# An FFN whose half-size weight sums move from VectorE to accumulating transfers of GpSimd

## The chip, the cores and the metric

The kernel runs on one core of one Trainium2 chip. The metric is the device time of one execution in microseconds (us). Before the change, three runs took 1903.16, 1903.44 and 1905.04 us; the median is 1903.44 us.

## The reference, cut to what matters

Two layers, each of which runs a half-step FFN, a set of token mixers and a second half-step FFN on a residual stream `x` of 512 tokens by 1024 features, all in float32. Only the FFN is touched by the change:

```
def swiglu(h, w_in, w_out):
    gate, up = jnp.split(h @ w_in, 2, axis=-1)
    return (jax.nn.silu(gate) * up) @ w_out

x = x + 0.5 * swiglu(rms_norm(x, ffn1_norm[l]), ffn1_w_in[l], ffn1_w_out[l])   # w_in 1024 x 5632, w_out 2816 x 1024
x = x + ...                                                                    # token mixers
x = x + 0.5 * swiglu(rms_norm(x, ffn2_norm[l]), ffn2_w_in[l], ffn2_w_out[l])
```

So there are four FFNs in an execution: first and second FFN of layer 0, first and second FFN of layer 1.

## The kernel before, in words

**Precision.** Every large product is made of three multiplications in a reduced float32 format (fp32r): each operand is split into a rounded part ("hi") and the rest ("lo"), and `mm3` (L208, L212, L213) adds hi·hi, hi·lo and lo·hi. A weight tile is split by `parted`: ScalarE (ACT) casts it to hi (L196), VectorE (DVE) subtracts to get lo (L197). The split tiles `hl` rotate through three buffers, so a split can start when the product three places earlier has ended.

**The FFN's stages.** The 22 blocks of 128 hidden features are taken in chunks of 8, 8 and 6 (`CHUNKS`). For each chunk the kernel computes the hidden activations `hh`, `hl` and then streams `w_out` rows (granules `st`, two buffers) to add the chunk's part of the output into `xT`. In the first chunk of an FFN, `cover` computes 6 blocks (4 in the first FFN of layer 1) with plain products, straight from the unnormalised x; meanwhile `halves_of_x` prepares seven combinations of quarters of the normalised x (tiles `xc`, from `xn` and `T`). From then on `halved` computes the remaining blocks two at a time, as a **pair**, with seven half-size products in the place of eight (the Strassen-Winograd scheme). This makes 12 `halved` stages, of 1 or 2, 4 and 3 pairs: 33 pairs in all. The four stages of an FFN's first chunk are called the **openings** here; they start while `cover`'s last results are still being finished (`finish`: L434 to L440).

**A pair.** A pair needs four quarters of `w_in`, 128 x 1024 floats (512 KB) each, called q0 (gate columns, first half of rows; `a11`), q1 (gate, second half; `a12`), q2 (up, first half; `a21`), q3 (up, second half; `a22`). `load` brings them from HBM with four DMAs on SyncE's queue (SP, L510) into tiles `w`, whose tags `x0`..`x3` and `x4`..`x7` alternate from pair to pair; in an opening the same tags hold the split x that `cover` still multiplies with, so each load starts when `cover` has done with its tag. `combine` makes four sums of quarters on DVE (L529) in tiles `S` (three buffers):

```
1: lambda: (a21, a22, ALU.add),
2: lambda: (s(1), a11, ALU.subtract),
3: lambda: (a11, a21, ALU.subtract),
4: lambda: (a12, s(2), ALU.subtract),
```

The seven products run in the order P1, P2, P6, P5, P7, P3, P4; their weights are q0, q1, sum 2, sum 1, sum 3, sum 4, q3. Each is 24 multiplications of 128 x 128 by 128 x 256. `prepare` splits the weights of a product two products ahead (`LEAD = 2`). Sums 1 and 2 of the next pair are made in the steps P7 and P3, sums 3 and 4 just before their own splits. The results leave PSUM by ACT copies (L583, L589, L592), DVE adds (L585, L594, L596) and `y`, `hh`, `hl` (L602 to L605).

**What sets the order.** The framework's scheduler places instructions on each engine by a simulated time, so the order on a queue need not be that of the source; each engine, and each of the queues SP and GpSimd (POOL), then runs its own list strictly in order. POOL does almost nothing in the kernel before: a few memsets and 16 small DMAs (`og`, `qkg`, `fb`, `cw`, L672 to L678) at the start of the mixers.

Of the kernel before, what the change touches and what calls it, by code (L numbers as in the profile page):

```python
# [8 lines left out]
F32 = mybir.dt.float32  # L9
# [4 lines left out]
AF = mybir.ActivationFunctionType  # L14
ALU = mybir.AluOpType
# [8 lines left out]
P = 128  # L24
# [3 lines left out]
KD = D // P  # L28
FF = 2816
# [15 lines left out]
class Trunk:  # L45
# [268 lines left out]
    def ffn(self, w_in, w_out, next_gain, covered, begin=None, out=None):  # L314
# [5 lines left out]
        with tc.tile_pool(name=self.n("ffn"), bufs=1) as fp:  # L320
# [3 lines left out]
            for f0, nf in CHUNKS:  # L324
# [5 lines left out]
                ]  # L330
                halved = self.halved(fp, w_in, f0 + (covered if f0 == 0 else 0), f0 + nf, f0)
                finish = self.cover(fp, w_in, covered, begin, halved) if f0 == 0 else None
                for n, _ in enumerate(halved):

                    if f0 == 0 and n == 0:
                        finish()
# [105 lines left out]
    def halves_of_x(self, fp):  # L442


        nc = self.nc
        H = T // 2
        xn = []
        for q in range(4):
            xq = fp.tile([P, 2, T], F32, tag=("hh2", "hl2", "hh3", "hl3")[q], name=self.n("xn"))
            for i in range(2):  # L450
                k = 2 * q + i
                nc.vector.scalar_tensor_tensor(  # L452
                    out=xq[:, i, :], in0=self.xT[:, k, :], scalar=self.gain[:, k : k + 1],
                    in1=self.inv, op0=ALU.mult, op1=ALU.mult,
                )
            xn.append(xq)

        quarter = lambda a, b: [xn[2 * a + i][:, :, b * H : (b + 1) * H] for i in range(2)]
        both = lambda t: [t[:, 2 * i : 2 * i + 2, :] for i in range(2)]

        def minus(out, a, b):
            for o, u, v in zip(out, a, b):
                nc.vector.tensor_sub(o, u, v)
            return out

        self.xc = {}

        def part(name, src):
            c = len(self.xc)
            hi, lo = (  # L470
                fp.tile([P, 4, H], F32R, tag=f"x{w}{c}", name=self.n("xc")) for w in "hl"
            )
            for h, l, u in zip(both(hi), both(lo), src):
                nc.scalar.copy(h, u)
                nc.vector.tensor_sub(l, u, h)  # L475
            self.xc[name] = hi, lo

        b11, b12, b21, b22 = (quarter(a, b) for a in range(2) for b in range(2))
        yield part("P1", b11)
        yield part("P2", b21)  # L480
        t1 = both(fp.tile([P, 4, H], F32, tag="S", name=self.n("T"), bufs=3))
        minus(t1, b12, b11)

        t2 = minus(b11, b22, t1)
        yield part("P6", t2)
        yield part("P5", t1)
        yield part("P7", minus(b12, b22, b12))
        yield part("P3", b22)
        yield part("P4", minus(b21, b21, t2))

    def halved(self, fp, w_in, fa, fb, f0):

        nc = self.nc
        H = T // 2
        ORDER = ("P1", "P2", "P6", "P5", "P7", "P3", "P4")  # L500
        steps = [(f, p) for f in range(fa, fb, 2) for p in ORDER]
        raw, sums, parts = {}, {}, {}

        def load(f):
            for q in range(4):
                t = self.res.tile(
                    [P, 4, 2 * P], F32, tag=f"x{4 * ((f - fa) // 2 % 2) + q}", name=self.n("w")
                )
                c = (q // 2) * FF + f * P
                nc.sync.dma_start(  # L510
                    t,
                    w_in[(q % 2) * 512 : (q % 2) * 512 + 512, c : c + 2 * P].rearrange(
                        "(k p) c -> p k c", p=P
                    ),
                )
                raw[f, q] = t

        def combine(f, name):
            a11, a12, a21, a22 = (raw[f, q] for q in range(4))
            s = lambda i: sums[f, i]  # L520

            t = s(2) if name == 4 else fp.tile([P, 4, 2 * P], F32, tag="S", name=self.n("S"), bufs=3)
            a, b, op = {
                1: lambda: (a21, a22, ALU.add),
                2: lambda: (s(1), a11, ALU.subtract),
                3: lambda: (a11, a21, ALU.subtract),
                4: lambda: (a12, s(2), ALU.subtract),
            }[name]()
            nc.vector.tensor_tensor(t, a, b, op=op)  # L529
            sums[f, name] = t  # L530

        def prepare(f, p):
            a11, a12, a21, a22 = (raw[f, q] for q in range(4))
            if p in ("P7", "P3"):
                combine(f, 3 if p == "P7" else 4)
            src = {
                "P1": a11, "P2": a12, "P6": sums.get((f, 2)), "P5": sums.get((f, 1)),
                "P7": sums.get((f, 3)), "P3": sums.get((f, 4)), "P4": a22,
            }[p]
            hi, lo = self.parted(src.rearrange("p k c -> p (k c)"), skew=SKEW_HELD)  # L540
            parts[f, p] = [a.rearrange("p (k c) -> p k c", k=4) for a in (hi, lo)]

        def product(f, p, bank, first, last, parted):
            hi, lo = parts.pop((f, p))
            xh, xl = self.xc[p]
            for i in range(2):
                acc, c = bank[:, i * H : (i + 1) * H], slice(i * P, (i + 1) * P)
                for k in range(4):
                    self.mm3(
                        acc, hi[:, k, c], lo[:, k, c], xh[:, k, :], xl[:, k, :],  # L550
                        first and i == 0 and k == 0, last and i == 1 and k == 3,
                        parted and i == 0 and k == 0,
                    )

        tmp = lambda tag: fp.tile([P, T], F32, tag=tag, name=self.n(tag), bufs=2)
        LEAD = 2
        load(fa)
        for f, p in steps[:LEAD]:
            prepare(f, p)
        yield  # L560
        for n, (f, p) in enumerate(steps):
            if p == "P1" and f == fa:
                combine(f, 1)
                combine(f, 2)
            if n + LEAD < len(steps):
                prepare(*steps[n + LEAD])
            if f + 2 < fb:
                if p == "P1":
                    load(f + 2)
                elif p in ("P7", "P3"):  # L570
                    combine(f + 2, 1 if p == "P7" else 2)
            if p == "P1":
                self.ntog += 1
                a, b, c = (
                    self.bank(t) for t in (("mm", "mm", "mm"), ("sc", "sc", "pt"))[self.ntog % 2]
                )
            product(
                f, p, {"P2": c, "P5": b, "P3": b}.get(p, a), p in ("P1", "P2", "P5"),
                p in ("P2", "P3", "P4"), n == 0,
            )  # L580
            if p == "P1":
                g1 = tmp("g1")
                nc.scalar.copy(g1, a)  # L583
            elif p == "P2":
                nc.vector.tensor_add(g1, g1, c)  # L585
                self.act(g1, g1, AF.Silu)
            elif p == "P6":
                g2 = tmp("g2")
                nc.scalar.copy(g2, a)  # L589
            elif p == "P5":  # L590
                u2 = tmp("u2")
                nc.scalar.copy(u2, b)  # L592
            elif p == "P7":
                nc.vector.tensor_add(u2, u2, a)  # L594
            elif p == "P3":
                nc.vector.tensor_add(g2, g2, b)  # L596
                self.act(g2, g2, AF.Silu)
            else:
                q = (f - f0) // 2
                pair = lambda t: t.rearrange("p (i t) -> p i t", i=2)  # L600
                y = fp.tile([P, 2, T], F32, tag="S", name=self.n("y"), bufs=3)
                nc.vector.tensor_mul(y[:, :, H:], pair(g2), pair(u2))  # L602
                nc.vector.tensor_mul(y[:, :, :H], pair(g1), pair(a))
                nc.scalar.copy(self.hh[q], y)
                nc.vector.tensor_sub(self.hl[q], y, self.hh[q])  # L605
            yield
# [722 lines left out]
```

## Time and profile before

| what | value |
|---|---|
| the profiled execution's own time | 1903.5 us |
| its span (first to last instruction) | 1901.7 us |
| granted TensorE clock | 1.0 |
| PE busy | 1877.0 us (99%) |
| DVE busy | 1390.4 us (73%) |
| ACT busy | 928.7 us (49%) |
| POOL busy | 27.4 us (1%) |
| moved by DMA | 185.63 MB, mean 98 GB/s |

The profiled execution lies 0.06 us from the median of the runs. An engine's busy time is the union of its instructions; for PE the ends of multiplications are modelled, so that its idle gaps are real, but being busy is not being at full speed. "Idle before" in a group of instructions is idle time of that engine just ahead of them, with what ended it.

### The profile page before, as it was taken

How to read it: one execution, taken by the hardware profiler on the slowest of the kernel's cores; microseconds unless marked ns; L12 is line 12 of the kernel's file. 1: busy time of each engine (PE TensorE's matmuls, PEld its weight loads, DVE VectorE, ACT ScalarE, POOL GpSimd, SP SyncE). 2: the span in 40 equal slices, each digit the busy share in tenths (PEclk: the TensorE clock that was granted, in tenths of full speed). 3: DMA queues.
4: the chain of work that ended last, by engine and by line, in shares of the span. 5: the costliest groups of instructions: out<-in, count | busy, mean ns of one | idle time of the engine just before them, and what ended most of it. 6: DMA issues, size and time to landing. Idle time of an engine off the chain costs nothing.

```text
span 1901.7 us, 30176 instructions
## 1 busy us (share of the span) xinstructions
PE 1877.0 (99%) x12240; PEld 1679.9 (88%) x12240; DVE 1390.4 (73%) x2004; ACT 928.7 (49%) x1418; POOL 27.4 (1%) x56
## 2 busy tenths in 40 slices
PE   8999999999999999999999999999999999999999
PEld 6889989899877788989989899998998787899897
DVE  7958757678787884857689486676868878768483
ACT  4525425464666542534555253455546665335252
POOL 0000000100000000000000000001000000000000
PEclk9999999999999999999999999999999999999999
DMA  5442421232323362341244334113323234424302
GB/s 144 145 150 72 145 76 36 73 96 69 77 76 93 99 197 80 100 142 37 73 144 139 100 100 133 45 56 78 91 62 87 78 107 131 159 68 126 106 23 89
DMA packets 176059, 185.63 MB, mean 98 GB/s; under 512 B 17680, under 2 KB 148752, under 8 KB 175920
## 3 DMA queue, kind: packets, MB, share of 16 engines
q1 hardware_dynamic: 175408, 183.69, 32.4%
q8 instruction: 96, 1.57, 0.3%
q14 instruction: 43, 0.35, 0.1%
q0 software_dynamic: 512, 0.02, 0.1%
HBM read 176.27 MB, written 2.10 MB: 94 GB/s over the span
## 4 chain that ended last, share of the span: by engine, by line
PE 84%; DVE 11%; ACT 3%; issue 2%; DMA 0%; SPq 0%; DVEq 0%; ACTq 0%
PE mm L208 13%; PE mm L213 13%; PE mm L212 13%; PE sc L208 8%; PE sc L212 8%; PE sc L213 8%; PE pt L208 4%; PE pt L212 4%; PE pt L213 4%; DVE hl L197 2%; DVE xc L475 2%; PE po L208 1%; PE po L213 1%; PE po L212 1%; DVE xn L452 1%
## 5 line engine op out<-in xcount | busy, mean ns | idle before, releaser
L197 DVE TENSOR_TENSOR hl<-st,hl 128x512 fp32r<-128x512 f32 (+2 forms) x268 | 254.8, 952 | 221.5 <-ACT hl L196 220.5
L196 ACT CAST hl<-st 128x512 fp32r<-128x512 f32 (+2 forms) x268 | 222.4, 832 | 379.0 <-PE pt L213 131.3
L213 PE MATMUL mm<-xc,hl 128*128 128x256 f32 x952 | 263.1, 277 | 2.2 <-DVE hl L197 2.2
L208 PE MATMUL mm<-xc,hl 128*128 128x256 f32 (+1 forms) x958 | 263.5, 276 | 1.7 <-ACT hl L196 1.7
L212 PE MATMUL mm<-xc,hl 128*128 128x256 f32 x952 | 263.1, 276 | 0.0
L208 PE MATMUL sc<-xc,hl 128*128 128x256 f32 (+1 forms) x774 | 212.4, 276 | 0.0
L212 PE MATMUL sc<-xc,hl 128*128 128x256 f32 x768 | 212.3, 276 | 0.0
L213 PE MATMUL sc<-xc,hl 128*128 128x256 f32 x768 | 212.1, 276 | 0.0
L196 ACT CAST hl<-S 128x1024 fp32r<-128x1024 f32 x132 | 138.7, 1051 | 140.1 <-DVE S L529 61.2
L197 DVE TENSOR_TENSOR hl<-w,hl 128x1024 fp32r<-128x1024 f32 x99 | 121.3, 1225 | 110.8 <-ACT hl L196 110.8
L197 DVE TENSOR_TENSOR hl<-S,hl 128x1024 fp32r<-128x1024 f32 x132 | 161.2, 1222 | 29.4 <-ACT hl L196 29.2
L208 PEld LDWEIGHTS mm<-xc,hl 128*128 128x128 f32 x958 | 179.8, 188 | 2.8 <-ACT hl L196 2.3
L213 PEld LDWEIGHTS mm<-xc,hl 128*128 128x128 f32 x952 | 178.6, 188 | 2.9 <-DVE hl L197 2.8
L212 PEld LDWEIGHTS mm<-xc,hl 128*128 128x128 f32 x952 | 178.7, 188 | 0.0
L196 ACT CAST hl<-w 128x1024 fp32r<-128x1024 f32 x99 | 103.9, 1050 | 143.4 <-PE po L213 52.7
L208 PEld LDWEIGHTS sc<-xc,hl 128*128 128x128 f32 x774 | 145.3, 188 | 0.5
L212 PEld LDWEIGHTS sc<-xc,hl 128*128 128x128 f32 x768 | 144.2, 188 | 0.0
L213 PEld LDWEIGHTS sc<-xc,hl 128*128 128x128 f32 x768 | 144.2, 188 | 0.0
L208 PE MATMUL mm<-hl,x 128*128 128x256 f32 (+1 forms) x384 | 112.4, 293 | 0.7 <-DVE qk L1105 0.4
L208 PE MATMUL mm<-x,hl 128*128 128x512 f32 x272 | 109.9, 404 | 0.0
L213 PE MATMUL mm<-hl,x 128*128 128x256 f32 (+1 forms) x384 | 107.5, 280 | 0.0
L212 PE MATMUL mm<-hl,x 128*128 128x256 f32 (+1 forms) x384 | 107.3, 279 | 0.0
(407 smaller groups left out, 4640.5 us busy)
## 6 DMA issues: line engine op xcount, KB each, us to landing
w<-in_ffn_w_in_dram SPq DMA_DIRECT2D x132, 512.0 KB, 3.6
st<-in_ffn_w_out_dram SPq DMA_DIRECT2D x88, 512.0 KB, 3.4
st<-in_ffn_w_in_dram SPq DMA_DIRECT2D x88, 256.0 KB, 3.2
st<-in_w_mix_in_dram SPq DMA_DIRECT2D x88, 256.0 KB, 2.7
st<-in_w_mix_out_dram SPq DMA_DIRECT2D x24, 256.0 KB, 2.8
st<-in_w_mix_in_dram SPq DMA_DIRECT2D x32, 128.0 KB, 2.3
xs<-in_x_dram SPq DMA_DIRECT2D x8, 256.0 KB, 5.5
QB<-QA SPq DMA_DIRECT2D x16, 128.0 KB, 2.3
```

Source lines behind the costliest of these rows:

```text
L196: a = nc.scalar.copy(hi, src[:, c : c + w])
L197: b = nc.vector.tensor_sub(lo, src[:, c : c + w], hi)
L208: nc.tensor.matmul(acc[:, c], ah, bh[:, c], start=first and c.start == 0, stop=False, skip_group_check=True,)
L212: nc.tensor.matmul(acc, ah, bl, start=False, stop=False, skip_group_check=True)
L213: nc.tensor.matmul(acc, al, bh, start=False, stop=last, skip_group_check=True)
L452: nc.vector.scalar_tensor_tensor(out=xq[:, i, :], in0=self.xT[:, k, :], scalar=self.gain[:, k : k + 1], in1=self.inv, op0=ALU.mult, op1=AL ...
L475: nc.vector.tensor_sub(l, u, h)
```

## The change

Three of the four sums of a pair are made by transfers that GpSimd issues with `accum_op=ALU.add`: the transfer reads its source and adds it to what the destination holds. `load` brings the quarters in the order q2, q3, q0, q1 and then has q3 read once more from HBM and added onto the tile of q2 (sum 1: q2 + q3). `second` is the one sum left on DVE (tile `S`): that sum + q0. `third` reads q2 once more from HBM and adds it onto the tile of q0, after q0 has been split for P1 and read by `second`. `fourth` adds the tile `S` onto the tile of q1, after q1 has been split for P2 (from SBUF to SBUF).

As these transfers can only add, signs are moved into x: the first four of the eight blocks of x in `halves_of_x` are multiplied by a negated gain (`ngain`, one small ACT instruction for each FFN), two of its combinations change their form, and three ACT copies out of PSUM get a factor of -1. The products, their order, the DMAs of `load` (but for their order) and everything outside the four FFNs stay as they are. `combine` goes, and with it three of four L529 instructions.

```diff
         xn = []
+        self.ngain = self.const.tile([P, KD], F32, tag="ngain", name=self.n("ngain"))
+        nc.scalar.activation(self.ngain, self.gain, AF.Copy, scale=-1.0)
...
-                    out=xq[:, i, :], in0=self.xT[:, k, :], scalar=self.gain[:, k : k + 1],
+                    out=xq[:, i, :], in0=self.xT[:, k, :],
+                    scalar=(self.ngain if k < 4 else self.gain)[:, k : k + 1],
...
-        t2 = minus(b11, b22, t1)
+        t2 = minus(b11, b22, t1, ALU.add)
...
-        yield part("P7", minus(b12, b22, b12))
+        yield part("P7", neither(b12, b12, b22))
...
         def load(f):
-            for q in range(4):
+            for q in (2, 3, 0, 1):
...
-        def combine(f, name):
...
+            nc.gpsimd.dma_start(raw[f, 2], quarter(f, 3), accum_op=ALU.add)
+
+        def second(f):
+            t = sums[f] = fp.tile([P, 4, 2 * P], F32, tag="S", name=self.n("S"), bufs=3)
+            nc.vector.tensor_add(t, raw[f, 2], raw[f, 0])
+
+        def third(f):
+            nc.gpsimd.dma_start(raw[f, 0], quarter(f, 2), accum_op=ALU.add)
+
+        def fourth(f):
+            nc.gpsimd.dma_start(raw[f, 1], sums[f], accum_op=ALU.add)
+
         def prepare(f, p):
-            if p in ("P7", "P3"):
-                combine(f, 3 if p == "P7" else 4)
             src = {
-                "P1": a11, "P2": a12, "P6": sums.get((f, 2)), "P5": sums.get((f, 1)),
-                "P7": sums.get((f, 3)), "P3": sums.get((f, 4)), "P4": a22,
+                "P1": raw[f, 0], "P2": raw[f, 1], "P6": sums.get(f), "P5": raw[f, 2],
+                "P7": raw[f, 0], "P3": raw[f, 1], "P4": raw[f, 3],
             }[p]
...
             if p == "P1" and f == fa:
-                combine(f, 1)
-                combine(f, 2)
+                second(f)
+            if p == "P1":
+                third(f)
+                fourth(f)
...
-                elif p in ("P7", "P3"):
-                    combine(f + 2, 1 if p == "P7" else 2)
+                elif p == "P7":
+                    second(f + 2)
...
-                nc.scalar.copy(g1, a)
+                nc.scalar.activation(g1, a, AF.Copy, scale=-1.0)
```

The same replacement of a copy by a copy times -1 is made for `g2` and `u2`.

More of the change, by code (lines that the diff above doesn't have):

```diff
@@ L459, in halves_of_x, with minus, neither @@
         both = lambda t: [t[:, 2 * i : 2 * i + 2, :] for i in range(2)]
-        def minus(out, a, b):
+        def minus(out, a, b, op=ALU.subtract):
             for o, u, v in zip(out, a, b):
-                nc.vector.tensor_sub(o, u, v)
+                nc.vector.tensor_tensor(o, u, v, op=op)
+            return out
+        def neither(out, a, b):
+            for o, u, v in zip(out, a, b):
+                nc.vector.scalar_tensor_tensor(
+                    out=o, in0=u, scalar=-1.0, in1=v, op0=ALU.mult, op1=ALU.subtract
+                )
             return out
@@ L502, in halved, with quarter @@
         raw, sums, parts = {}, {}, {}
+        def quarter(f, q):
+            c = (q // 2) * FF + f * P
+            return w_in[(q % 2) * 512 : (q % 2) * 512 + 512, c : c + 2 * P].rearrange(
+                "(k p) c -> p k c", p=P
+            )
         def load(f):
-            for q in range(4):
+            for q in (2, 3, 0, 1):
                 t = self.res.tile(
@@ L508, in load @@
                 )
[L509 to L515, printed above, removed]
-                raw[f, q] = t
-        def combine(f, name):
[L519 to L530, printed above, removed]
+                nc.sync.dma_start(t, quarter(f, q))
+                raw[f, q] = t
+            nc.gpsimd.dma_start(raw[f, 2], quarter(f, 3), accum_op=ALU.add)
[6 more added lines that the diff above has]
+            nc.gpsimd.dma_start(raw[f, 1], sums[f], accum_op=ALU.add)
         def prepare(f, p):
-            a11, a12, a21, a22 = (raw[f, q] for q in range(4))
-            if p in ("P7", "P3"):
-                combine(f, 3 if p == "P7" else 4)
             src = {
-                "P1": a11, "P2": a12, "P6": sums.get((f, 2)), "P5": sums.get((f, 1)),
-                "P7": sums.get((f, 3)), "P3": sums.get((f, 4)), "P4": a22,
+                "P1": raw[f, 0], "P2": raw[f, 1], "P6": sums.get(f), "P5": raw[f, 2],
+                "P7": raw[f, 0], "P3": raw[f, 1], "P4": raw[f, 3],
             }[p]
@@ L588, in halved @@
                 g2 = tmp("g2")
-                nc.scalar.copy(g2, a)
+                nc.scalar.activation(g2, a, AF.Copy, scale=-1.0)
             elif p == "P5":
                 u2 = tmp("u2")
-                nc.scalar.copy(u2, b)
+                nc.scalar.activation(u2, b, AF.Copy, scale=-1.0)
             elif p == "P7":
```

## The prediction

> **What bounds the kernel now.** I read the page's busy times first, then the windows of the `halved` stages, then what PE waited for inside the openings, then DVE's timeline there, then the transfers.
>
> The page's first two engines, and the three groups of the sums (columns: count, busy us, mean ns, idle before):
>
> ```profile
> PE 1877.0 (99%) x12240; PEld 1679.9 (88%) x12240; DVE 1390.4 (73%) x2004; ACT 928.7 (49%) x1418; POOL 27.4 (1%) x56
> L529 DVE TENSOR_TENSOR S<-w,w 128x1024 f32<-128x1024 f32 x66 | 80.5, 1220 | 6.6 <-DMA w<-in_ffn_w_in_dram 6.1
> L529 DVE TENSOR_TENSOR S<-S,w 128x1024 f32<-128x1024 f32 x33 | 40.4, 1223 | 0.8
> L529 DVE TENSOR_TENSOR S<-w,S 128x1024 f32<-128x1024 f32 x33 | 40.3, 1220 | 0.3
> ```
>
> PE idles 24.7 us in all. The sums are 132 instructions, 161.2 us of DVE, 4.9 us for each of 33 pairs.
>
> The windows of an opening with one pair, a stage of four pairs, the opening with two pairs, and the two other openings (length, then busy us with counts of PE, PEld, DVE, ACT, POOL; clock, DMA share, GB/s):
>
> ```profile
> 82.10:105.00 22.90, 20.42 (x170) 19.47 (x169) 21.32 (x26) 12.56 (x17) 0.00 (x0) 1.00 0.50 156
> 148.60:224.90 76.30, 76.30 (x674) 76.26 (x674) 64.25 (x64) 42.11 (x51) 0.00 (x0) 1.00 0.34 104
> 684.40:703.60 19.20, 19.20 (x171) 19.16 (x170) 17.03 (x21) 12.18 (x16) 0.00 (x0) 1.00 0.62 191
> 1001.30:1041.50 40.20, 38.76 (x339) 38.33 (x338) 36.69 (x41) 22.92 (x29) 0.00 (x0) 1.00 0.46 144
> 1620.90:1640.00 19.10, 19.10 (x170) 19.09 (x169) 16.83 (x20) 12.16 (x16) 0.00 (x0) 1.00 0.61 194
> ```
>
> Four pairs take 76.3 us, 19.07 each, with PE never idle: a pair is 7 x 24 = 168 multiplications, which the timeline starts every 0.113 us (19.04 us), so a product takes 2.72 us. DVE is 84% busy there and still hidden. The eight later stages and the openings at 684 and 1621 all run at this pace. Only two openings are slower: 22.9 - 19.1 = 3.8 us lost at 82 us, and 40.2 - 38.1 = 2.1 us at 1001 us. So all that DVE's relief can win is 5.9 us. What PE waited for in these two (us, times, longest):
>
> ```profile
> PE mm L208 <- ACT hl L196: 1.7, 2, 1.4
> PE mm L213 <- DVE hl L197: 0.8, 1, 0.8
> ...
> PE mm L213 <- DVE hl L197: 1.4, 1, 1.4
> ```
>
> Behind these splits stands DVE, which has no gap in this stretch of the first opening:
>
> ```profile
> 90.71 0.68 DVE L440 TENSOR_TENSOR hl<-ui,hh 128x512 fp32r<-128x512 f32 x1
> 91.32 0.68 DVE L434 TENSOR_TENSOR gi<-pt,inv 128x512 f32<-128x512 f32 x1
> 91.92 0.68 DVE L585 TENSOR_TENSOR g<-g,mm 128x512 f32<-128x512 f32 x1
> 92.51 1.22 DVE L529 TENSOR_TENSOR S<-w,w 128x1024 f32<-128x1024 f32 x1
> 93.65 0.69 DVE L437 TENSOR_TENSOR ui<-gi,ui 128x512 f32<-128x512 f32 x1
> 94.25 1.22 DVE L529 TENSOR_TENSOR S<-w,S 128x1024 f32<-128x1024 f32 x1
> ```
>
> Sums 3 and 4 come at 92.5 and 94.2, while P7 was due at 82.1 + 4 x 2.72 = 93.0. The transfers (KB, median us to landing), and the SP queue's share of the 16 DMA engines:
>
> ```profile
> w<-in_ffn_w_in_dram SPq DMA_DIRECT2D x132, 512.0 KB, 3.6
> st<-in_w_mix_in_dram SPq DMA_DIRECT2D x32, 128.0 KB, 2.3
> cw<-in_conv_w_dram POOLq DMA_DIRECT2D x6, 1.0 KB, 3.3
> og<-in_hgrn_out_gain_dram POOLq DMA_DIRECT2D x4, 0.2 KB, 2.8
> q1 hardware_dynamic: 175408, 183.69, 32.4%
> ```
>
> **The change, part by part.** *Removed:* 99 of 132 sums, 99 x 1.22 = 121 us of DVE, 3.7 us a pair. In the 30 pairs at full pace this is worth nothing; in the two slow openings up to -3.8 and -2.1 us.
>
> *Nothing:* the negated copies are copies still (0.59 us each, off PE's path), the changed forms in `halves_of_x` are the same number of DVE instructions of the same size (0.60 us each for L463, 0.6 to 0.68 for L452). `ngain` is 8 columns, some 0.2 us of ACT by the 0.20 us of a 4-column activation, four times; in ACT's list two of the four stand just after the load of a gain that lands 4.4 us after its issue at 55.31 and 978.98, which could hold ACT for half a microsecond while it has idle gaps of 2 us. If the cover went, about 1 us. The loads' new order (q2, q3, q0, q1) changes SP's list at full pace alone, where each load has most of a pair to spare; in the openings the list still runs in the order in which `cover` frees the tags.
>
> *Added:* 99 accumulating transfers of 512 KB on POOL's queue, 66 from HBM and 33 from SBUF. No such transfer is in the trace; let L be the time from issue to landing. From below: a tiny POOL transfer lands in 2.8 us, and 512 KB instead of 128 KB cost SP 3.6 - 2.3 = 1.3 us, for the whole 512 KB some 1.7; L = 4.5 if adding is free. From above: in the crowd at the opening of 684 us a 512 KB load took 6.0 us (issued 672.68, landed 678.69); twice the data beyond a base of 2 us, and half a microsecond of POOL for the issue (the small ones hold it 0.52 to 0.73 us), make about 10. I take 7 where the queues are quiet and 9 in the crowd: nearer to the slow end, as the destination has to be read too. POOL's own issue time is 0.7 or, for more pieces, perhaps 2 us.
>
> The Trainium skill says (Collectives: The Full Stack, "The bandwidth ceiling") that a reduction in the DMA engines runs at half the rate of a copy because it reads two sources. No run here shows it; by that rule alone 1.8 us of data would become 3.5, and L about 6.3, which would make the sum below some 4 us lower.
>
> *Deadlines in full pace.* Take the second pair of the stage at 148.6, which starts at 167.7. `third` may go once P1's lo is made (DVE, 164.9); P7 starts at 178.6 and needs the cast (1.05) and the lo (1.22) just before, so landing is due at about 176.4: 11.5 us. `fourth` may go at 167.6 and is due at 179.1: again 11.5. The accumulation of `load` stands ahead of them in POOL's list (the scheduler puts that of the next pair but one first) and has a whole pair of slack. With L = 7 to 9 all is hidden: cost 0. What a late landing would hold: ACT's cast for P7, and behind it in order the `u2` copy and the casts of P3 and P4; on DVE the lo's behind these.
>
> *Opening at 82 us.* `third` is listed behind the accumulation for the next stage's second pair, whose q2 load takes the place of a load issued at 81.6 and landing in 4.1 to 4.6 us. So POOL is held until 86, `third` goes at about 87, and lands 7 + 1 us later (the data ahead of it), at 95. Cast and lo end at 97.3; P7's third multiplication was due at 93.2. Stall 4.1 instead of 3.8: +0.3. `fourth`, one microsecond behind, is covered by P7's own 2.7 us.
>
> *Opening at 1001 us.* `second` ends at 1002.7 as sum 1 did; `third` goes then, lands at 1009.8, due 1010.1. No stall: -2.1.
>
> *Openings at 684 and 1621 us.* They lost nothing before, and here the new transfer stands on the path: q2 is issued at 672.20 and lands at about 678, its accumulation takes L = 9 to 687, `second` ends at 688.2. On DVE the lo of P2 is listed right behind `second`: 689.4, due 684.4 + 2.72 + 0.2 = 687.4. Stall 2.0. `third` goes at 688.3 and lands at 697.3; lo at 699.6, due 684.4 + 10.9 + 0.2 + 2.0 = 697.5. Stall 2.1 more. Some 4 us each: +8.
>
> *Sum:* 0.3 - 2.1 + 8 = +6. The profiled execution (1903.5, span 1901.7) is as good as the median, so 1903.5 + 6 = 1909.5. Each microsecond of L is worth about 1 in the opening at 82, 1 in that at 1001 and 2 in each of the others (once for P2, once more for P7), 6 in all upwards: L two higher gives about 1922. Downwards it ends sooner: L two lower gives 0 in the crowded openings, -1.7 and -2.1 in the others, 1899.7.
>
> **Rivals.** *The transfers are quick* (L of 5 or less): the openings at 684 and 1621 stay whole, that at 1001 gains 2.1, that at 82 about 3: 1898.5. For it: the SP loads' 3.6 us, and DMA engines only 34% busy at full pace. Against: the openings, where it counts, show 61 to 62%. Chance 0.24.
>
> *In between*, within 0.2% (3.8 us, about what a measurement of this kernel can tell from no change): 0.18.
>
> *The transfers miss full pace as well.* The SP queue's 32.4% of 1901.7 us for 183.69 MB makes 1.76 us of all 16 engines for 512 KB: 7.0 us a pair now, and 12.3 to 17.6 with three more of them at one to two passes, out of 19.07. At three passes the engines would need 22.8 us, 3.8 too many in the 12 pairs beyond the two that are loaded ahead in each later stage: +46. Or by latency: beyond L = 11.5 each microsecond is paid in 21 pairs (33 less the first of each stage); L = 13 gives 32 us, and the openings 20: about 1955. Chance 0.24.
>
> *The change does not do what it says:* POOL's list holds the 99 transfers and DVE's 33 sums, so no chance is given to it.
>
> **How the numbers follow.** The forecast case, 1907.3 to about 1922, has 0.34. Slower by over 0.2%: 0.34 + 0.24 = 0.58; within: 0.18; faster: 0.24. The range runs from 1898, the quick end, to 1950, which takes in some 0.4 of the rival that misses full pace; about 0.16 is left out. The forecast's own range is 1907 to 1922.
>
> **What would show it.** DVE's busy time falls by some 120 us, to about 1270. L529's groups become one of 33; POOL shows 99 new transfers. Right: stages of four pairs still take 76.3 us; the openings at 684 and 1621 show PE waiting for DVE L197 or ACT L196, some 4 us each, with DVE's `second` or ACT's cast waiting for a DMA onto `w`; the opening near 1001 is shorter than 40.2. Wrong in size: landings of 5 us and openings at 19.1. Wrong in kind: a stage of four pairs longer than 76.3, ACT's L196 on `w` waiting for POOL's transfers in every pair.

## The result, and the profile after

The changed kernel took 1919.94 us (median of four runs, 1915.45 to 1920.73) beside 1903.3 us for the kernel before in the same comparison: ratio 1.0081, 95% interval 1.0063 to 1.0098, slower by 16.6 us. Its profiled execution is the shortest of the four, 1915.45 us (span 1913.7), 12.0 us over the profiled one of before. So the profiles below show 12.0 of the 16.6 us; where the other executions spent some 4 us more is not shown.

The page's first part, after:

```profile
PE 1879.9 (98%) x12240; PEld 1683.8 (88%) x12240; DVE 1280.2 (67%) x1905; ACT 928.9 (49%) x1422; POOL 142.3 (7%) x155
```

DVE is relieved: 110 us less. Of its four groups of sums one is left, 40.3 us in the place of 161.2 (from here on, groups with their shapes kept apart: count, busy us, mean ns, idle before):

```profile
L537 DVE TENSOR_TENSOR S<-w,w 128x1024 f32<-128x1024 f32 x33 | 40.3, 1220 | 32.5 <-DMA w<-in_ffn_w_in_dram 32.5
```

The sums are 120.9 us less, the engine 110.2: its timeline starts an instruction some 0.08 us before the one ahead has ended, and busy time counts that once, which is much of the difference. What is new is the 32.5 us of waiting for a transfer in front of `second`, where all the sums of before waited 7.7 us. POOL's new groups, and the transfers on the page (KB, median us to landing; packets, MB, share of 16 DMA engines):

```profile
L532 POOL DMA_DIRECT2D w<-in_ffn_w_in_dram x33 | 44.5, 1349 | 643.7 <-DMA w<-in_ffn_w_in_dram 334.8 <-PE pt L213 159.8 <-DVE hl L440 109.2
L541 POOL DMA_DIRECT2D w<-in_ffn_w_in_dram x33 | 43.0, 1303 | 509.4 <-DVE hl L197 483.2 <-DVE S L537 16.4 <-DMA w<-in_ffn_w_in_dram 9.8
L545 POOL DMA_DIRECT2D w<-S x33 | 31.3, 949 | 63.7 <-DVE hl L197 63.7
```

```profile
q1 hardware_dynamic: 175408, 183.69, 31.6%
q0 software_dynamic: 40112, 51.93, 16.9%
...
w<-in_ffn_w_in_dram SPq DMA_DIRECT2D x132, 512.0 KB, 5.1
...
w<-in_ffn_w_in_dram POOLq DMA_DIRECT2D x66, 512.0 KB, 6.8
...
w<-S POOLq DMA_DIRECT2D x33, 512.0 KB, 6.0
```

An issue holds POOL for 0.95 to 1.35 us on average. An accumulating transfer takes 16.9% x 1913.7 / 99 = 3.27 us of all 16 engines, against 1.73 for a plain load (q1's 31.6%, shared out by bytes), and the plain loads land 1.5 us later than before (5.1 for 3.6).

The windows of the first opening, a stage of four pairs, and the other three openings (length, then busy us of PE, PEld, DVE, ACT, POOL; clock, DMA share, GB/s):

```profile
81.70:108.80 27.10, 21.04 (x171) 20.81 (x171) 18.44 (x23) 12.36 (x17) 4.82 (x4) 0.87 0.91 213
152.30:228.60 76.30, 76.30 (x674) 76.28 (x673) 52.10 (x53) 42.33 (x51) 11.70 (x10) 1.00 0.82 188
688.50:710.80 22.30, 20.15 (x170) 19.70 (x169) 17.67 (x21) 11.86 (x16) 4.78 (x4) 1.00 0.97 229
1008.50:1052.70 44.20, 40.51 (x338) 40.06 (x337) 30.60 (x35) 22.66 (x29) 8.27 (x7) 0.96 0.92 210
1631.80:1652.10 20.30, 19.92 (x171) 19.70 (x170) 17.70 (x21) 11.94 (x16) 4.80 (x4) 1.00 1.05 247
```

The stage of four pairs is as long as before, 76.3 us, with the DMA share up from 0.34 to 0.82. From the first multiplication to the last one the openings grew by 4.0, 3.1, 4.0 and 1.1 us: together 12.2, all of what the profiled executions differ by. (I go on calling them the openings at 82, 684, 1001 and 1621 us.) What PE waited for in the span, among others:

```profile
PE mm L208 <- ACT g L603: 7.0, 4, 6.1
PE mm L213 <- DVE hl L197: 5.3, 2, 3.4
```

**The 6.1 us, in the opening at 82.** POOL's timeline (start, us), then ACT's:

```profile
85.37 1.29 POOL L532 DMA_DIRECT2D w<-in_ffn_w_in_dram  x1 [9.65 <-DVE ui L435]
86.12 1.86 POOL L541 DMA_DIRECT2D w<-in_ffn_w_in_dram  x1
86.87 2.02 POOL L545 DMA_DIRECT2D w<-S  x1
```

```profile
95.85 1.04 ACT L196 CAST hl<-w 128x1024 fp32r<-128x1024 f32 x1 [7.46 <-DMA w<-in_ffn_w_in_dram]
96.80 0.61 ACT L439 CAST hh<-ui 128x512 fp32r<-128x512 f32 x1
97.32 0.62 ACT L152 ACTIVATE g<-g 128x512 f32<-128x512 f32 x1
97.85 0.61 ACT L152 ACTIVATE gi<-gi 128x512 f32<-128x512 f32 x1
98.37 0.57 ACT L603 ACTIVATE g<-mm 128x512 f32<-128x512 f32 x1
```

The accumulation for the next stage's second pair stands first on POOL, `third` behind it. The three go 0.75 us apart, but by the trace they land 6.25, 9.65 and 11.8 us after their issue: one behind the other. ACT's cast for P7 waits for `third` until 95.85, and behind that cast, in order, stands the copy (L603) that frees the PSUM bank into which P7's first multiplication writes. PE stands still from 92.8 to 98.9.

**The 3.4 us, in the opening at 1001.** POOL's timeline, then DVE's:

```profile
1010.38 1.28 POOL L541 DMA_DIRECT2D w<-in_ffn_w_in_dram  x1 [8.55 <-DVE S L537]
1011.13 1.45 POOL L545 DMA_DIRECT2D w<-S  x1
1012.16 1.75 POOL L532 DMA_DIRECT2D w<-in_ffn_w_in_dram  x1
```

```profile
1023.71 1.22 DVE L537 TENSOR_TENSOR S<-w,w 128x1024 f32<-128x1024 f32 x1 [2.87 <-DMA w<-in_ffn_w_in_dram]
1024.85 0.68 DVE L440 TENSOR_TENSOR hl<-ui,hh 128x512 fp32r<-128x512 f32 x1
1025.45 1.22 DVE L197 TENSOR_TENSOR hl<-w,hl 128x1024 fp32r<-128x1024 f32 x1
```

The instruction at 1023.71 is `second` of the second pair, whose products are the last 19.1 us of the opening, from about 1033.6 on. Its sum 1 was the third accumulation in a row on the queue (issued 1012.16, landed 1023.69), and the lo of P3 stands behind it. L213's other wait, 1.8 us, is the same thing at 684 us, with the lo of P2 behind `second`:

```profile
691.18 1.23 DVE L537 TENSOR_TENSOR S<-w,w 128x1024 f32<-128x1024 f32 x1 [9.98 <-DMA w<-in_ffn_w_in_dram]
692.33 1.22 DVE L197 TENSOR_TENSOR hl<-w,hl 128x1024 fp32r<-128x1024 f32 x1
```

**Half clock.** With both long stalls comes a stretch in which TensorE had half its clock (the last column but two); the windows around the first, where it begins during the stall:

```profile
95.00:99.00 4.00, 0.00 (x1) 0.00 (x1) 2.07 (x3) 3.15 (x6) 0.00 (x0) 0.55 0.75 162
99.00:102.20 3.20, 3.20 (x15) 3.20 (x16) 2.52 (x4) 2.83 (x4) 1.30 (x1) 0.50 0.70 180
```

15 multiplications in 3.2 us where 28 fit: some 1.5 us more, and about as much again after the stall at 1023.

### The profile page after: what moved, and what is told of

Read it like the earlier page. It is cut to its first block, busy times and chain, and to the rows that moved or that the text cites. A ratio compares the mean times of both kernels' runs of the same rounds, so it can differ in the third digit from the quotient of the medians.

```text
span 1913.7 us, 30445 instructions
## 1 busy us (share of the span) xinstructions
PE 1879.9 (98%) x12240; PEld 1683.8 (88%) x12240; DVE 1280.2 (67%) x1905; ACT 928.9 (49%) x1422; POOL 142.3 (7%) x155
## 3 DMA queue, kind: packets, MB, share of 16 engines
q1 hardware_dynamic: 175408, 183.69, 31.6%
q0 software_dynamic: 40112, 51.93, 16.9%
## 4 chain that ended last, share of the span: by engine, by line
PE 83%; DVE 8%; DMA 4%; ACT 3%; issue 2%; SPq 0%; POOL 0%; POOLq 0%; ACTq 0%; DVEq 0%
PE mm L208 13%; PE mm L213 13%; PE mm L212 13%; PE sc L208 8%; PE sc L212 8%; PE sc L213 8%; PE pt L208 4%; PE pt L212 4%; PE pt L213 4%; DMA w<-in_ffn_w_in_dram 3%; PE po L208 2%; PE po L213 2%; PE po L212 2%; DVE hl L197 1%; DVE xc L487 1%
## 5 line engine op out<-in xcount | busy, mean ns | idle before, releaser
L197 DVE TENSOR_TENSOR hl<-w,hl 128x1024 fp32r<-128x1024 f32 x198 | 242.6, 1226 | 228.6 <-ACT hl L196 228.4
L196 ACT CAST hl<-w 128x1024 fp32r<-128x1024 f32 x198 | 207.0, 1045 | 195.1 <-PE po L213 52.7
L213 PE MATMUL mm<-xc,hl 128*128 128x256 f32 x952 | 265.0, 278 | 5.3 <-DVE hl L197 5.3
L213 PE MATMUL sc<-xc,hl 128*128 128x256 f32 x768 | 212.1, 276 | 0.0
L213 PEld LDWEIGHTS mm<-xc,hl 128*128 128x128 f32 x952 | 180.3, 189 | 5.8 <-DVE hl L197 5.7
L213 PEld LDWEIGHTS sc<-xc,hl 128*128 128x128 f32 x768 | 144.2, 188 | 0.0
L208 PE MATMUL mm<-x,hl 128*128 128x512 f32 x272 | 109.6, 403 | 0.0
L213 PE MATMUL mm<-hl,x 128*128 128x256 f32 (+1 forms) x384 | 107.7, 280 | 0.0
L213 PE MATMUL mm<-x,hl 128*128 128x512 f32 x272 | 106.4, 391 | 0.0
L212 PE MATMUL mm<-x,hl 128*128 128x512 f32 x272 | 105.9, 389 | 0.0
```

Of the source, the lines that this page charges most:

```text
L196: a = nc.scalar.copy(hi, src[:, c : c + w])
L197: b = nc.vector.tensor_sub(lo, src[:, c : c + w], hi)
L208: nc.tensor.matmul(acc[:, c], ah, bh[:, c], start=first and c.start == 0, stop=False, skip_group_check=True,)
L212: nc.tensor.matmul(acc, ah, bl, start=False, stop=False, skip_group_check=True)
L213: nc.tensor.matmul(acc, al, bh, start=False, stop=last, skip_group_check=True)
```

## The experiments

All but e6, which repeats the changed kernel, are versions of it in which a condition BY decides, for sum n of pair f, between the transfer (`add`) and DVE (in place, 1.22 us); in e3 to e5 BY is always true and `add` itself is changed. `f0` is 0 in an FFN's first chunk. The first, shortened:

```diff
+        def BY(n, f): return f0 > 0        # openings (f0 == 0): DVE
...
-            nc.gpsimd.dma_start(raw[f, 2], quarter(f, 3), accum_op=ALU.add)
+            if BY(1, f): add(raw[f, 2], quarter(f, 3))
         def second(f):
+            if not BY(1, f): nc.vector.tensor_add(raw[f, 2], raw[f, 2], raw[f, 3])
...
+            if p == "P7" and not BY(3, f): nc.vector.tensor_sub(raw[f, 0], sums[f], raw[f, 3])
+            if p == "P3" and not BY(4, f): nc.vector.tensor_add(raw[f, 1], raw[f, 1], sums[f])
...
+                if BY(3, f): third(f)
+                if BY(4, f): fourth(f)
```

All results together; openings and four-pair stages in us from the first multiplication of `halved` to the start of the last one, in the profiled execution (0.1 to 0.3 less than a window around them):

| kernel | median us | ratio to before (95%) | 82 | 684 | 1001 | 1621 | four pairs |
|---|---|---|---|---|---|---|---|
| before | | | 22.8 | 19.0 | 40.1 | 19.0 | 76.1 |
| changed | 1919.94 | 1.0081 (1.0063 to 1.0098) | 26.8 | 22.1 | 44.0 | 20.1 | 76.1 |
| changed, again (e6) | 1918.01 | 1.0078 (1.0063 to 1.0093) | 28.6 | 22.0 | 42.4 | 21.4 | 76.1 |
| e1 openings by DVE | 1904.63 | 1.0009 (1.0000 to 1.0018) | 22.8 | 19.0 | 40.2 | 19.0 | 76.1 |
| e2 openings only | 1912.16 | 1.0047 (1.0032 to 1.0062) | 21.2 | 23.9 | 45.9 | 22.8 | 76.1 |
| e3 order of the program | 1934.38 | 1.0156 (1.0133 to 1.0179) | 22.7 | 22.7 | 45.1 | 23.9 | 77.9 to 80.7 |
| e4 plain copies | 1903.29 | 1.0004 (0.9995 to 1.0013) | 23.3 | 19.0 | 38.6 | 19.0 | 76.1 |
| e5 twice | 2130.11 | one run | 39.0 | 39.7 | 64.3 | 38.6 | 101.2 to 103.5 |
| e7 sum 1 by DVE | 1909.28 | 1.0032 (1.0018 to 1.0045) | 26.8 | 19.4 | 42.4 | 20.7 | 76.1 |
| e8 sum 1 only | 1915.73 | 1.0057 (1.0040 to 1.0074) | 23.4 | 25.1 | 39.0 | 26.5 | 76.1 |
| m1 | 1902.35 | 0.9991 (0.9982 to 1.0000) | 23.4 | 19.0 | 39.2 | 19.0 | 76.1 |
| m2 | 1901.92 | 0.9986 (0.9977 to 0.9995) | 22.9 | 19.4 | 38.7 | 19.0 | 76.1 |

The profiled executions of e2, e7 and e8 are the longest of theirs (1917.73, 1912.00, 1916.65 us): their openings are upper ends, and what a kernel costs is read from the median. From here on, a stall is the time between the starts of two multiplications beyond the usual 0.113 us; that is 0.16 us more than the idle time which the views give for it.

### e1: transfers at full pace alone

> The three sums are made by DVE again (in place, 1.22 us each) for the pairs of the four chunks that a covered opening precedes (5 of 33 pairs), and by accumulating transfers for the other 28. Theory 1 (all of the loss lies in the four openings, full pace hides the transfers): the openings take 22.9, 19.2, 40.2 and 19.1 us as before, stages of four pairs 76.3, and the time is 1902 to 1905. Rival (the transfers cost a little everywhere, in clock or in engine time, beyond the 12.3 us found in the openings, since the other executions of the changed kernel were 4 us longer than the profiled one): 1907 or more, with a granted clock under 1.00 in the late stages.

Measured 1904.63 us. Windows of the opening at 82, of that at 1001 and of a stage of four pairs:

```profile
81.70:104.50 22.80, 20.34 (x170) 19.39 (x168) 21.22 (x25) 12.55 (x17) 2.74 (x2) 1.00 0.74 186
...
1001.60:1041.90 40.30, 38.84 (x338) 38.39 (x337) 36.58 (x41) 22.95 (x29) 2.59 (x2) 1.00 0.61 161
...
148.30:224.50 76.20, 76.20 (x675) 76.20 (x674) 52.15 (x53) 42.33 (x51) 11.71 (x10) 1.00 0.81 190
```

84 of the 99 transfers stay, and the cost goes to 1.7 us, inside what can be told from none (its interval just reaches none). So the loss needs the transfers in the openings. The negated gain, the changed forms of x and the loads' new order are all still in e1, so these cost no more than that either.

### e2: transfers in the openings alone

The condition is `f0 == 0`.

> The opposite half: accumulating transfers for the 5 pairs of the openings alone, DVE sums (in place) for the 28 pairs at full pace. Theory 1: the time of the changed kernel, 1915 to 1920, with openings of about 27, 22, 44 and 20 us. Rival (cost everywhere): a good part of the loss is gone, 1911 or less.

1912.16 us, between the two: three of the openings are longer than in the changed kernel, but that at 82 takes 21.2 us, 1.6 less than before the change. There POOL has nothing in front of `third`:

```profile
85.54 1.28 POOL L528 DMA_DIRECT2D w<-in_ffn_w_in_dram  x1 [10.20 <-issue]
86.29 1.44 POOL L528 DMA_DIRECT2D w<-S  x1
```

It lands at 91.69 in the place of 95.77. So "only in the openings" was too simple: in the first one the loss comes from a transfer for the next stage, a full-pace one, that goes first.

### e3: POOL's list in the order of the program

```diff
         def add(t, a):
-            nc.gpsimd.dma_start(t, a, accum_op=ALU.add)
+            i = nc.gpsimd.dma_start(t, a, accum_op=ALU.add)
+            self.follow('p', i)            # order only, no wait
```

> All transfers stay; the accumulating ones alone are held in the order of the program on POOL's list, so that in the opening at 82 us sums 3 and 4 no longer stand behind the accumulation for the next pair. If that place in the list is what makes the opening 27.0 us: sum 3 goes at 84.7 instead of 86.1 and finds an empty queue, lands at 91 instead of 95.8, the opening takes 19.5 to 21 us and the stretch of half clock after it is gone; in the two-pair opening sum 1 of the second pair comes after sums 3 and 4 of the first as it did, so 44 us stay there or become longer. In all 1908 to 1913. If the reads from HBM are slow by themselves in the openings, whatever stands ahead, sum 3 still lands at 94 or later and the opening stays over 25 us: 1914 to 1920.

1934.38 us: outside all that was expected. `third` at 82 did go at 84.94 and land at 91.18, and that opening fell from 26.8 to 22.7 (two stalls of 1.4 and 0.5 us, then half clock again). But full pace broke: the accumulation that feeds the third pair's `second` now stands behind `third` and `fourth` of the second pair and is issued at 167.76, 0.6 us after that pair began, where in the changed kernel it went 9.3 us before. DVE and ACT there:

```profile
175.77 1.23 DVE L546 TENSOR_TENSOR S<-w,w 128x1024 f32<-128x1024 f32 x1 [2.93 <-DMA w<-in_ffn_w_in_dram]
176.91 0.68 DVE L614 TENSOR_TENSOR g<-g,mm 128x512 f32<-128x512 f32 x1
```

```profile
177.63 0.63 ACT L152 ACTIVATE g<-g 128x512 f32<-128x512 f32 x1 [3.77 <-DVE g L614]
178.17 0.58 ACT L618 ACTIVATE g<-mm 128x512 f32<-128x512 f32 x1
```

`second` waits, behind it the sum of g1, behind that ACT's Silu, and behind the Silu the copy that frees P7's bank. Stages of four pairs grow by 1.8 to 4.6 us and those of three by 1.6 to 2.1: 20.6 us in all, which with 13.5 in the openings makes about the 33.3 us between the profiled executions.

### e4: plain copies in the place of accumulations

```diff
-            nc.gpsimd.dma_start(t, a, accum_op=ALU.add)
+            nc.gpsimd.dma_start(t, a)
```

> Every accumulating transfer becomes a plain copy of the same bytes from the same queue: the three additions are left out, all waits and the list of POOL are kept. If the accumulation itself (3.27 us of all 16 engines for 512 KB, against 1.73 for a plain load) is what makes the openings late: engine time falls to 1.7 to 1.9 us for each, landing from 6.0 to about 4.5 us, the openings come to about 21, 19.2, 39 and 19.1 us and the time to 1899 to 1904. If it is the chain (load, then a transfer that waits for it, then DVE, then another transfer) and POOL's list, whatever the transfer does: landing falls little, and openings of 25 and 42 us stay: 1910 or more.

1903.29 us. From the page:

```profile
q0 software_dynamic: 14768, 51.93, 8.0%
...
w<-in_ffn_w_in_dram POOLq DMA_DIRECT2D x66, 512.0 KB, 4.6
...
w<-S POOLq DMA_DIRECT2D x33, 512.0 KB, 3.1
```

With the same bytes, list and waits, a transfer takes 8.0% x 1900.5 / 99 = 1.54 us of the engines, less than half, and lands 2.2 to 2.9 us sooner. The openings at 684 and 1621 are whole again and that at 1001 is 1.5 us shorter than before, most of the gain foreseen there. At 82 `third` still stands behind the other transfer and lands at 92.00: 23.3 us, a miss of 2 us. The plain copies also go in fewer packets, 14768 for 40112; but SyncE's plain loads, whose packets are smaller still (175408 for 183.69 MB), take 1.73 us, so small packets alone do not make 3.27. The cost is thus the accumulation's own duration, and only at 82 the list as well.

### e5: every accumulation twice

```diff
+            for _ in range(2):
                 nc.gpsimd.dma_start(t, a, accum_op=ALU.add)
```

> Every accumulating transfer is made twice, one behind the other, so that the three sums come out wrong; nothing else is changed. It tests how much room full pace has. By the changed kernel's rows a pair needs 4 x 1.73 us of all 16 engines for its loads and 3 x 3.27 for its accumulations, 16.7 of 19.07 us; with six it is 26.6. Theory (full pace hides the transfers only as long as the engines are not full): the stages of four pairs become longer than 76.3 us, towards 26.6 us for each pair that is not loaded ahead, the three-pair ones longer than 57.2, over 50 us in all: 1970 or more. Rival (landing counts and the engines do not: two overlap at little cost): landings of 7 to 9 us, stages of four pairs stay at 76.3, and only the openings grow, to some 1935.

2130.11 us. A window of four pairs has the DMA engines full:

```profile
163.90:267.20 103.30, 87.01 (x674) 84.80 (x673) 51.92 (x53) 41.68 (x51) 24.69 (x22) 0.92 0.99 198
```

103.3 us for four pairs is near the 4 x 26.6 = 106 us of engine time worked out beforehand. So full pace hides three accumulations but not six; the rival that latency alone counts is out.

### e6: the changed kernel again

> The changed kernel as it is, once more, on the chip and beside the runs of the kernel before that the next two share, for a second profile: its other executions were 4 to 5 us longer than the profiled one. If only the openings vary (by the stretch of half clock after a stall): stages of four pairs at 76.3 again, the opening at 684 or 1621 longer by some 3 us with such a stretch in it, and 1915 to 1921. If something else varies, the openings come to 27, 22, 44 and 20 us again and the rest of the span grows.

1918.01 us. Four pairs take 76.3 us again; the first opening is 1.8 us longer than in the first profile, that at 1001 is 1.6 shorter (a stall of 3.5 us there, but no half clock after it), that at 1621 is 1.3 longer. So the openings vary by 1 to 2 us each. The longer executions were not profiled. The mean granted clocks of these four, 0.998 for the profiled one and 0.997, 0.996 and 0.994 for those of 1918.00, 1918.01 and 1920.89 us, speak for more half clock; but in the first measurement two executions that were 4 and 5 us longer than the profiled one have its clock, 0.997. Where their time went stays open.

### e7 and e8: sum 1, or sums 3 and 4

Conditions: `f0 > 0 or n != 1` and `f0 > 0 or n == 1`.

> In the 5 pairs of the openings DVE makes sum 1 (in place, 1.22 us), transfers make sums 3 and 4; in the other 28 pairs transfers make all three. If it is the transfer of sum 1 that costs (it waits for a load, DVE's sum 2 waits for it, sum 3 stands behind its like on POOL): the openings come to about 21.2, 19.7, 38.5 and 19.7 us and the time to 1899 to 1903. If it is sum 3, whose cast stands in front of a PSUM copy in ACT's list: 22 to 24, 21, 40 and 21, some 1906 to 1909.

> The other half: in the 5 pairs of the openings a transfer makes sum 1, DVE sums 3 and 4; transfers make all three in the other 28. If the transfer of sum 1 costs: about 21.5, 21, 41 and 19.8 us in the openings, with DVE's sum 2 waiting for a transfer in the last three, and 1904 to 1908. If sum 3 costs: openings as with DVE alone or better, 21.5, 19.2, 39 and 19.1, and 1901 to 1903.

Neither came out as either theory had it. In e7 (1909.28 us) the opening at 684 is nearly whole (19.4), but at 82 `third` still goes behind the other transfer (86.06 and 87.30, landing at 96.76): 26.8 us. In e8 (1915.73 us) the opening at 1001 is 1.1 us shorter than before, but those at 684 and 1621 are longer than in the changed kernel. DVE at 684 in e8:

```profile
687.51 1.23 DVE L545 TENSOR_TENSOR S<-w,w 128x1024 f32<-128x1024 f32 x1 [9.97 <-DMA w<-in_ffn_w_in_dram]
688.77 1.22 DVE L557 TENSOR_TENSOR w<-S,w 128x1024 f32<-128x1024 f32 x1
689.92 1.22 DVE L197 TENSOR_TENSOR hl<-w,hl 128x1024 fp32r<-128x1024 f32 x1
```

The wait for sum 1 is the same, but the scheduler put sum 3 (L557) ahead of P2's lo: stalls of 3.3 us here and 4.1 at 1621, each with 6.8 us of half clock, most of it behind the stall. So sum 1 costs most in the openings at 684 and 1621 (without its transfer, in e7, 0.4 and 1.7 us over the kernel before are left there), sums 3 and 4 in those at 82 and 1001 (without theirs, in e8, +0.6 and -1.1). Each version is scheduled anew, and the parts do not add up.

### m1 and m2: transfers only where there is room

In the openings at 82 and 1001 alone (`early`); all other sums by DVE.

```diff
# m1
+            return self.early and f0 == 0 and (n == 4 or n == 1 and f == fa)
# m2
+            return self.early and f0 == 0 and (n != 1 or f == fa)
```

> Transfers only where the runs so far show room for them: in the two openings before which the kernel before lost time (82 and 1001 us), sum 4 of every pair and sum 1 of the first pair by an accumulating transfer, everything else, full pace and the other two openings included, by DVE. If what the transfers can give is DVE's relief there, with no transfer on the path: about 21 and 38.5 us instead of 22.8 and 40.1, 19.0 in the other two, 1899 to 1901. If the relief only uncovers the next wait (the cast of sum 3 on ACT, 1.4 us after it): 22.5 and 40, and 1902 to 1904, no change.

> As the kernel that goes with it, but sum 3 of these three pairs by a transfer too, with nothing ahead of it on the queue: it goes at 85 and lands at 91.5, 1.4 us before P7 is due. If the landing decides: 21.2 us at 82 (as where only the openings had transfers), 39 to 40 at 1001, about 1900. If half clock follows the remaining stall of 1 to 2 us, 2 us more: 1902.

Windows of m2:

```profile
81.80:104.90 23.10, 21.55 (x171) 21.15 (x170) 19.41 (x23) 12.46 (x17) 2.21 (x2) 0.93 0.80 203
...
1001.50:1040.30 38.80, 38.57 (x338) 38.33 (x337) 31.25 (x35) 22.60 (x29) 4.38 (x4) 1.00 0.81 202
```

m1 (1902.35 us) came out nearest to its second case: 23.4 and 39.2 us in the two openings, and a time that cannot be told from the kernel before. m2 (1901.92 us) beats the changed kernel by far, and the kernel before by 2.1 us, which is little but clear of none (0.05 to 0.23%). 1.4 us of it is the opening at 1001. At 82 the stalls fell from 3.0 to 1.9 us, but a stretch of half clock (clock 0.93 in the window) took that back.

## Why the prediction was right or wrong, point by point

**Full pace at no cost: right, more narrowly than I said.** Four pairs take 76.3 us; within its stages the two transfers of a pair's beginning land 5.6 to 7.2 us after issue (median 6.1), due after 11.5 (e1 shows the same with full pace alone). But "a whole pair of slack" for the accumulation of `load` was wrong: in the changed kernel it lands 0.0 to 3.7 us before `second` reads it in the pairs loaded within a stage, and its place on POOL's list is all that gives that (e3). The rival that misses full pace was right in its mechanism; at 16.7 us of engine time per pair its condition was not met, at 26.6 (e5) it was. Its price by latency was set too low: the 20 us for the openings at L = 13 do not fit the rate of 6 us for each microsecond of L that the sum uses, by which they are some 34 (L is then 6 above the quiet 7 and 4 above the crowded 9).

**L of 7 and 9: about right where one transfer runs, too small in a row.** At full pace: 5.6 to 7.2 for `third` and `fourth`, 6.0 to 9.3 for the accumulation of `load`. In the crowd at 684: 9.29. As third in a row in the openings: 10.5 to 11.8. The Trainium skill's rule (Collectives: The Full Stack, "The bandwidth ceiling": a reduction in the DMA engines at half the rate of a copy) agrees with the trace: 3.27 us of engine time against 1.73 and 1.54, and the 6.3 us that it gave for L.

**Opening at 82, +0.3: the landing right, the cost wrong.** `third` was to go at 87 and land at 95; it went at 86.12 and landed at 95.77. The step that failed is what stands behind it. I let P7 begin in time and wait only for its split; in fact its first multiplication waited for a PSUM copy (L603) behind the blocked cast in ACT's list. The prediction had named such a copy (that of `u2`) behind this cast for full pace, but the sum for the opening did not use it. A stall of 6.2 us and half clock made it +4.0.

**Opening at 1001, -2.1: wrong by its sign.** I followed `third` of the first pair alone, which landed in 6.35 us. The step left out sum 1 of the second pair, third in the row on POOL, and `second` of that pair, which blocks DVE ahead of P3's lo. It cost +4.0. Most of the -2.1 was there to be had: e4 has -1.5, m2 -1.4.

**Openings at 684 and 1621, +4 each: mechanism right at 684, size too large.** The first landing was to come 2.6 us after the stage's start and came after 2.7 (688.5 to 691.16), and the stall of 2.0 measured 2.0 (1.8 of it idle). The second term, 2.1 for P7, measured 0.5 (0.3 idle): `third` found the queue quiet and took 5.92 us, not 9. At 1621 sum 1 landed in 7.4 us, in time for P2's lo; PE idled 0.4 us there, for the copy out of PSUM, and the opening cost 1.1 (in e6, 2.4).

**The sum.** +8 for two openings was +4.2, -1.8 for the other two was +8.0: 12.2 in place of 6, with one error in part against the other. The sign held, in part by the mechanism foreseen, but most of the loss lay in the openings where I had expected none. That the median, 1919.94, lies inside the forecast's own 1907 to 1922 is in good part luck: two thirds of the loss that the profile shows come from steps that the forecast did not have, and some 4 us of the median stand in no profile.

## What to carry to other kernels

Work moved from a busy engine to a transfer is free only while every transfer lands before the reader that is first *in line*: with in-order engines, look at what stands behind the blocked reader (here a PSUM copy, another product's split), not at the reader's own deadline. Count the transfers in a row on one queue, each with its full engine time, and those for later stages that the scheduler puts first. Where the relieved engine was hidden for most of the span, use such transfers only in the stages where it is not.

## What the runs showed of the hardware

**Half clock after short stalls.** In the `halved` stages of these profiles (e5 aside) there are 17 stretches of half clock, each of 3.41 or 6.83 us in the clock's record, and none appears away from a stall. They came with stalls of 1.9 to 6.9 us in all, and did not come with others of 1.6 to 3.5 (684 in the changed kernel, 1001 in e6, the opening at 82 before the change). Where a stall falls matters as much as its length. Within a profile the stretches begin whole multiples of 3.413 us apart (in the changed kernel at 95.38 and 1027.21, 273 of them). Windows cut along that grid, of the stall at 1001 in the changed kernel and of its like in e6:

```profile
1023.80:1027.21 3.41, 0.48 (x4) 0.48 (x5) 3.41 (x4) 0.35 (x1) 1.28 (x1) 1.00 0.45 74
1027.21:1030.63 3.42, 3.42 (x19) 3.42 (x18) 2.33 (x3) 0.00 (x0) 0.79 (x1) 0.50 1.16 247
```

```profile
1022.15:1025.56 3.41, 1.78 (x16) 1.58 (x14) 1.28 (x2) 2.45 (x3) 0.93 (x1) 1.00 0.84 254
1025.56:1028.97 3.41, 1.67 (x14) 1.68 (x15) 3.41 (x5) 0.00 (x0) 0.35 (x1) 1.00 0.73 95
1028.97:1032.39 3.42, 3.42 (x32) 3.42 (x31) 2.98 (x5) 1.58 (x2) 1.28 (x1) 1.00 1.11 312
```

In the first, 2.9 us of the stall lie in one piece of the grid, and the next piece has half clock; in e6 nearly the same stall is shared by two pieces, 1.6 and 1.7 us idle, and full clock goes on. So it is in all these stages: a piece at full clock with more than 1.8 us of idle PE was followed by half clock every time, one with less than 1.5 never, and those between went either way (2 of 10). The grid lies differently in every profile, so the same stall may cost some 1.5 us more or not. The Trainium skill (TensorE: Matmul & The Clock Gate, "The HAM clock gate") tells of a free-running window of about 3.4 us, with half rate after an idle one; the half rate and the window agree with the trace, but a window about half idle was enough here.

**Accumulating transfers hardly overlap.** Issued 0.75 us apart (the first opening, after) they land 4.2 and 2.9 us apart, around the 3.27 us that one takes of the engines.
